# The order of the last two chunks, and a last store in two halves, in a streamed binary cross-entropy

## The chip, the cores and the metric

The kernel runs on one core of one Trainium2 chip. The metric is the device time of one execution in microseconds (us). The kernel before takes 1886.61 us (median of 3 runs, 1886.12 to 1887.61).

## The reference

Binary cross-entropy, element by element, on two arrays of 8192 x 8192 float32. The target holds only 0 and 1.

```python
def reference(pred, target):
    eps = 1e-7
    pred = np.clip(pred, eps, 1 - eps)
    return -(target * np.log(pred) + (1 - target) * np.log(1 - pred))
```

Because the target is 0 or 1, the result is -log|clip(pred) + (target - 1)|, and this is what the kernel computes: one logarithm for each element. 537 MB are read and 268 MB written.

## The kernel before

The 67.1 million elements are seen as one flat stream and cut into 37 chunks (k = 0 to 36, `last` = 36). A chunk has 128 partitions, with `FIRST` = 8192 columns in chunk 0 and `WIDE` = 14336 columns in all others. A row of a chunk is contiguous in memory: 57344 bytes of float32.

There are two buffers on the chip. `ring_p` holds three chunks in float32: the prediction is loaded there, worked on in place, and stored from there as the result. `ring_t` holds one chunk of the target in bfloat16; the load narrows it on the way. So the prediction of chunk k + 2 can be loaded only when the store of chunk k - 1 has landed, and the target of chunk k + 1 only when the merges of chunk k are done.

Compute works on halves of a chunk (`PARTS` = 2, 7168 columns; below, 36a and 36b are the halves of chunk 36). For each half:

- `clip` (L85): one VectorE instruction bounds the prediction.
- `merge` (L91, L94, L95): VectorE adds target - 1; ScalarE takes the absolute value and then the logarithm, in place.
- `negate` (L99): VectorE multiplies by -1.

The order is written out by hand: each engine executes its instructions in the order in which the program emits them, and a wait of one of them holds up all that stand behind it on that engine. VectorE's order for a chunk is merge a, merge b of chunk k; negate a, negate b of chunk k; clip a, clip b of chunk k + 1. ScalarE has absolute value and logarithm of a, then of b.

All big transfers are issued by GpSimd (POOL), in one queue and in program order: `load_t(k + 1)` (L67), `store(k)` (L70), `load_p(k + 2)` (L63). A wait of one of them holds up the later ones. Only the first load of the prediction is issued by ScalarE.

The end is special. The target of chunk 36 is loaded in two halves, and `store(34)` is issued behind these two loads. `store(35)` comes after the negations of chunk 35. The last store, `store_last`, writes columns 0 to 13311 of chunk 36 by one transfer on POOL's queue (L74), and the last `REST` = 1024 columns by three transfers on SyncE's queue (L77), of 108, 12 and 8 rows.

Of the kernel before, what the change touches and what calls it, by code (L numbers as in the profile page):

```python
# [1 line left out]

# [4 lines left out]

EPS = 1e-7

WIDE = 14336  # L10
FIRST = 8192
SLOTS = 3
PARTS = 2
REST = 1024
ROWS = (108, 12, 8)


@with_exitstack
def kernel(
    ctx: ExitStack,  # L20
    tc: tile.TileContext,
    pred: bass.AP,
    target: bass.AP,
    out: bass.AP,
):
    nc = tc.nc
    fp32 = mybir.dt.float32
    bf16 = mybir.dt.bfloat16
    Alu = mybir.AluOpType
    Act = mybir.ActivationFunctionType  # L30
    P = nc.NUM_PARTITIONS

    R, C = pred.shape
    total = R * C // P
    n = (total - FIRST) // WIDE + 1
    assert FIRST + (n - 1) * WIDE == total
    widths = [FIRST] + [WIDE] * (n - 1)
    last = n - 1

    pool = ctx.enter_context(tc.tile_pool(name="rings", bufs=1))  # L40
    ring_p = pool.tile([P, SLOTS * WIDE], fp32, name="ring_p", tag="ring_p")
    ring_t = pool.tile([P, WIDE], bf16, name="ring_t", tag="ring_t")
    warm = pool.tile([1, 8], fp32, name="warm", tag="warm")

    def chunk(ap, k):
        flat = ap.rearrange("r c -> (r c)")
        start = sum(widths[:k]) * P
        return flat[start : start + widths[k] * P].rearrange("(p w) -> p w", p=P)

    def p_of(k, a=0, b=None):  # L50
        c = k % SLOTS * WIDE
        return ring_p[:, c + a : c + (widths[k] if b is None else b)]

    def t_of(k, a=0, b=None):
        return ring_t[:, a : widths[k] if b is None else b]

    def part(k, i):
        w = widths[k]
        return i * w // PARTS, (i + 1) * w // PARTS

    def load_p(k):
        queue = nc.scalar if k == 0 else nc.gpsimd
        queue.dma_start(out=p_of(k), in_=chunk(pred, k))  # L63

    def load_t(k, *cols):
        cols = cols or (0, widths[k])
        nc.gpsimd.dma_start(out=t_of(k, *cols), in_=chunk(target, k)[:, cols[0] : cols[1]])  # L67

    def store(k):
        nc.gpsimd.dma_start(out=chunk(out, k), in_=p_of(k))  # L70

    def store_last():
        w = WIDE - REST
        nc.gpsimd.dma_start(out=chunk(out, last)[:, :w], in_=p_of(last, 0, w))  # L74
        r = 0
        for rows in ROWS:
            nc.sync.dma_start(  # L77
                out=chunk(out, last)[r : r + rows, w:], in_=p_of(last, w)[r : r + rows, :]
            )
            r += rows  # L80
        assert r == P

    def clip(k, i):
        p = p_of(k, *part(k, i))
        nc.vector.tensor_scalar(  # L85
            out=p, in0=p, scalar1=EPS, scalar2=1 - EPS, op0=Alu.max, op1=Alu.min
        )

    def merge(k, i):
        p, t = p_of(k, *part(k, i)), t_of(k, *part(k, i))  # L90
        nc.vector.scalar_tensor_tensor(  # L91
            out=p, in0=t, scalar=1.0, in1=p, op0=Alu.subtract, op1=Alu.add
        )
        nc.scalar.activation(out=p, in_=p, func=Act.Abs)  # L94
        nc.scalar.activation(out=p, in_=p, func=Act.Ln)  # L95

    def negate(k, i):
        p = p_of(k, *part(k, i))
        nc.vector.tensor_scalar(out=p, in0=p, scalar1=-1.0, scalar2=None, op0=Alu.mult)  # L99

    with tc.manual_schedule():
        load_p(0)
        load_t(0)
        load_p(1)
        nc.vector.memset(warm, 1.0)  # L105
        nc.scalar.activation(out=warm, in_=warm, func=Act.Ln)  # L106
        for i in range(PARTS):
            clip(0, i)
        for k in range(n):
            for i in range(PARTS):  # L110
                merge(k, i)
            if k < last - 1:
                load_t(k + 1)
            elif k == last - 1:
                load_t(last, 0, WIDE // PARTS)
                load_t(last, WIDE // PARTS, WIDE)
                store(last - 2)
            for i in range(PARTS):
                negate(k, i)
            if k < last:  # L120
                for i in range(PARTS):
                    clip(k + 1, i)
            if k < last - 2:
                store(k)
            if k < last - 1:
                load_p(k + 2)
        store(last - 1)
        store_last()


# [1 line left out]
_INS = ['pred', 'target']  # L132
_OUTS = [((8192, 8192), 'float32')]


# [23 lines left out]
```

## Time and profile before

| | |
|---|---|
| time, median of 3 runs | 1886.61 us |
| the profiled execution: its time | 1888.07 us |
| the profiled execution: its span | 1886.3 us |
| VectorE (DVE) busy | 1117.8 us, 59% |
| ScalarE (ACT) busy | 901.3 us, 48% |
| GpSimd (POOL) busy | 279.0 us, 15% |
| data moved by DMA | 671.14 MB, mean 356 GB/s |
| one clip, one merge on VectorE, one negation (7168 columns) | 3.85, 7.5, 3.85 us |
| one ScalarE pass (7168 columns) | 6.1 us |
| a store of one chunk, issue to landing | 31.1 us |

Times in the profile are in us from the span's start. A line of the timeline gives start, duration, engine, source line (L91 is line 91 of the kernel), operation, output and input with shape and type, how many instructions are merged into the line, and in brackets how long the engine sat idle before it and who released it. A line of the table by windows gives the stretch and its length, the busy time of VectorE, ScalarE and POOL with the number of instructions, the clock, the mean busy share of the 16 DMA engines and the GB/s they moved. `SPq` is SyncE's queue. The profile also records each packet that a DMA engine moves, with its size, start and duration, and each completion that a transfer writes.

### The profile page before, as it was taken

Reading aid. Unit: us, or ns where it says so; the run is one execution under the profiler, and the core shown is the slowest. Engines: PE = TensorE matmul, PEld = TensorE weight load, DVE = VectorE, ACT = ScalarE, POOL = GpSimd, SP = SyncE. Lnnn points to the kernel's source line nnn. Section 1 sums busy time; section 2 is a strip of 40 time slices with the busy share of each in tenths; the row PEclk is TensorE's granted clock in tenths of the full one; section 3 lists DMA queues with packets and bytes.
Section 4 is the critical chain, followed back from the end, with each engine's and each line's share of the span. In section 5 each row is a group of like instructions: output and inputs, shape, how many; then the busy total and the mean of one; then the engine's idle time right before and its main releaser. Section 6 shows DMA issues by size and latency. Waiting matters only on the chain.

```text
span 1886.3 us, 684 instructions
## 1 busy us (share of the span) xinstructions
DVE 1117.8 (59%) x223; ACT 901.3 (48%) x150; POOL 279.0 (15%) x115
## 2 busy tenths in 40 slices
DVE  4675566565555665556665655556655566666571
ACT  3555544444445555554444444555555544444453
POOL 0120111111111111011111111111100111111000
DMA  9999999999999999999999999999999999999994
GB/s 328 342 370 370 374 364 350 354 360 354 350 361 356 352 364 375 371 373 372 360 353 364 351 353 360 356 351 358 366 371 371 376 368 362 361 351 354 355 361 189
DMA packets 16293, 671.14 MB, mean 356 GB/s; under 512 B 1824, under 2 KB 1824, under 8 KB 1952
## 3 DMA queue, kind: packets, MB, share of 16 engines
q0 software_dynamic: 15984, 666.38, 98.4%
q10 hardware_dynamic: 144, 4.19, 0.6%
q1 hardware_dynamic: 160, 0.52, 0.1%
q14 instruction: 5, 0.04, 0.0%
HBM read 536.87 MB, written 268.44 MB: 427 GB/s over the span
## 4 chain that ended last, share of the span: by engine, by line
DMA 64%; issue 30%; DVE 2%; ACT 1%; POOL 1%; POOLq 0%; DVEq 0%; PEldq 0%
DMA ring_t<-in_target_dram 64%; DVE ring_p L91 2%; ACT ring_p L95 1%; ACT ring_p L94 1%; POOL out_dram L70 0%; DVE ring_p L99 0%; POOL ring_p L63 0%; POOLq L154 0%; POOLq L67 0%; POOL ring_t L67 0%; POOLq L70 0%; DVEq L91 0%; PEldq L154 0%; POOLq L74 0%
## 5 line engine op out<-in xcount | busy, mean ns | idle before, releaser
L94 ACT ACTIVATE ring_p<-ring_p 128x7168 f32<-128x7168 f32 (+1 forms) x74 | 451.4, 6100 | 952.0 <-DVE ring_p L91 952.0
L91 DVE SCALAR_TENSOR_TENSOR ring_p<-ring_t,ring_p 128x7168 f32<-128x7168 bf16 (+1 forms) x74 | 554.5, 7535 | 236.2 <-DMA ring_t<-in_target_dram 236.2
L99 DVE TENSOR_SCALAR ring_p<-ring_p 128x7168 f32<-128x7168 f32 (+1 forms) x74 | 285.0, 3851 | 486.5 <-ACT ring_p L95 486.5
L95 ACT ACTIVATE ring_p<-ring_p 128x7168 f32<-128x7168 f32 (+1 forms) x74 | 451.9, 6107 | 2.3
L85 DVE TENSOR_SCALAR ring_p<-ring_p 128x7168 f32<-128x7168 f32 (+1 forms) x74 | 281.6, 3847 | 19.4 <-DMA ring_p<-in_pred_dram 19.4
L70 POOL DMA_DIRECT2D out_dram<-ring_p x36 | 127.4, 3539 | 710.3 <-DVE ring_p L99 710.3
L67 POOL DMA_DIRECT2D ring_t<-in_target_dram x38 | 20.2, 531 | 830.8 <-DVE ring_p L91 830.0
L63 POOL DMA_DIRECT2D ring_p<-in_pred_dram x36 | 130.9, 3637 | 1.1 <-DMA out_dram<-ring_p 1.1
L74 POOL DMA_DIRECT2D out_dram<-ring_p x1 | 0.5, 531 | 40.1 <-DVE ring_p L99 40.1
L106 ACT ACT_TABLE_LOAD x1 | 1.3, 1283 | 1.1 <-PEq L143 1.1
L105 DVE MEMSET warm<- 1x8 f32 x1 | 0.1, 65 | 0.8 <-PEq L143 0.8
L106 ACT ACTIVATE warm<-warm 1x8 f32<-1x8 f32 x1 | 0.2, 207 | 0.0
L143 POOL MEMSET const-float32-0.0<- 128x1 f32 x1 | 0.1, 99 | 0.2 <-issue 0.2
L143 POOL MEMSET const-bfloat16-1.0<- 128x1 bf16 x1 | 0.1, 101 | 0.0
L143 POOL MEMSET const-uint8-127<- 128x1 uint8 x1 | 0.1, 99 | 0.0
L143 POOL MEMSET const-float32-1.0<- 128x1 f32 x1 | 0.1, 98 | 0.0
## 6 DMA issues: line engine op xcount, KB each, us to landing
ring_p<-in_pred_dram POOLq DMA_DIRECT2D x36, 7168.0 KB, 44.4
out_dram<-ring_p POOLq DMA_DIRECT2D x35, 7168.0 KB, 31.1
ring_t<-in_target_dram POOLq DMA_DIRECT2D x35, 3584.0 KB, 35.2
out_dram<-ring_p POOLq DMA_DIRECT2D x1, 6656.0 KB, 19.5
ring_p<-in_pred_dram ACTq DMA_DIRECT2D x1, 4096.0 KB, 19.5
out_dram<-ring_p POOLq DMA_DIRECT2D x1, 4096.0 KB, 21.3
ring_t<-in_target_dram POOLq DMA_DIRECT2D x2, 1792.0 KB, 17.9
ring_t<-in_target_dram POOLq DMA_DIRECT2D x1, 2048.0 KB, 21.4
```

The source lines that it names most:

```text
L63: queue.dma_start(out=p_of(k), in_=chunk(pred, k))
L67: nc.gpsimd.dma_start(out=t_of(k, *cols), in_=chunk(target, k)[:, cols[0] : cols[1]])
L70: nc.gpsimd.dma_start(out=chunk(out, k), in_=p_of(k))
L74: nc.gpsimd.dma_start(out=chunk(out, last)[:, :w], in_=p_of(last, 0, w))
L85: nc.vector.tensor_scalar(out=p, in0=p, scalar1=EPS, scalar2=1 - EPS, op0=Alu.max, op1=Alu.min)
L91: nc.vector.scalar_tensor_tensor(out=p, in0=t, scalar=1.0, in1=p, op0=Alu.subtract, op1=Alu.add)
L94: nc.scalar.activation(out=p, in_=p, func=Act.Abs)
L95: nc.scalar.activation(out=p, in_=p, func=Act.Ln)
L99: nc.vector.tensor_scalar(out=p, in0=p, scalar1=-1.0, scalar2=None, op0=Alu.mult)
L105: nc.vector.memset(warm, 1.0)
L106: nc.scalar.activation(out=warm, in_=warm, func=Act.Ln)
L143: nc = _bacc.Bacc("TRN2", target_bir_lowering=False, num_devices=1)
```

## The change

The loop over chunks ends two chunks earlier, with the same body. The last two chunks, 35 and 36, are written out:

- VectorE's order was: merge 35a, 35b; negate 35a, 35b; clip 36a, 36b; merge 36a, 36b; negate 36a, 36b. It becomes: merge 35a, 35b; clip 36a, 36b; negate 35a, merge 36a; negate 35b, merge 36b; negate 36a, 36b. ScalarE's order stays.
- POOL's order stays. `store(35)` now follows negate 35b in the new order.
- The last store's columns 0 to 13311 are written by two transfers instead of one: columns 0 to 7167, which wait for negate 36a, and columns 7168 to 13311, which wait for negate 36b. SyncE's three transfers are unchanged and wait for negate 36b.

The changed kernel has one line more above `clip`, so its line numbers from there on are higher by one.

```diff
     def store_last():
-        w = WIDE - REST
-        nc.gpsimd.dma_start(out=chunk(out, last)[:, :w], in_=p_of(last, 0, w))
+        half, w = WIDE // PARTS, WIDE - REST
+        for a, b in (0, half), (half, w):
+            nc.gpsimd.dma_start(out=chunk(out, last)[:, a:b], in_=p_of(last, a, b))
...
-        for k in range(n):
+        for k in range(last - 1):
             for i in range(PARTS):
                 merge(k, i)
-            if k < last - 1:
-                load_t(k + 1)
-            elif k == last - 1:
-                load_t(last, 0, WIDE // PARTS)
-                load_t(last, WIDE // PARTS, WIDE)
-                store(last - 2)
+            load_t(k + 1)
             for i in range(PARTS):
                 negate(k, i)
-            if k < last:
-                for i in range(PARTS):
-                    clip(k + 1, i)
+            for i in range(PARTS):
+                clip(k + 1, i)
             if k < last - 2:
                 store(k)
-            if k < last - 1:
-                load_p(k + 2)
+            load_p(k + 2)
+        for i in range(PARTS):
+            merge(last - 1, i)
+            load_t(last, *part(last, i))
+        store(last - 2)
+        for i in range(PARTS):
+            clip(last, i)
+        for i in range(PARTS):
+            negate(last - 1, i)
+            merge(last, i)
         store(last - 1)
+        for i in range(PARTS):
+            negate(last, i)
         store_last()
```

## Prediction

> **What bounds the kernel now.** I read the page first, then the timeline of the last 100 us, the table by windows of the tail, the transfers by issue, and the waits of SyncE's queue.
>
> ```profile
> DVE 1117.8 (59%) x223; ACT 901.3 (48%) x150; POOL 279.0 (15%) x115
> DMA  9999999999999999999999999999999999999994
> ```
>
> No compute engine is busy more than 59% of the span, and the DMA row is full in every slice but the last. The steady state is the DMA engines' own time, and the change does not touch it; what can change lies in that last slice (47 us). The timeline there:
>
> ```profile
> 1788.64 0.53 POOL L67 DMA_DIRECT2D ring_t<-in_target_dram  x1 [40.98 <-DVE ring_p L91]
> ...
> 1796.17 0.53 POOL L67 DMA_DIRECT2D ring_t<-in_target_dram  x1 [7.01 <-DVE ring_p L91]
> 1796.69 0.54 POOL L70 DMA_DIRECT2D out_dram<-ring_p  x1
> ...
> 1800.79 3.89 DVE L99 TENSOR_SCALAR ring_p<-ring_p 128x7168 f32<-128x7168 f32 x1 [4.92 <-ACT ring_p L95]
> ...
> 1813.07 3.90 DVE L99 TENSOR_SCALAR ring_p<-ring_p 128x7168 f32<-128x7168 f32 x1 [8.38 <-ACT ring_p L95]
> 1816.88 7.70 DVE L85 TENSOR_SCALAR ring_p<-ring_p 128x7168 f32<-128x7168 f32 x2
> 1817.26 3.62 POOL L70 DMA_DIRECT2D out_dram<-ring_p  x1 [20.03 <-DVE ring_p L99]
> 1824.50 15.14 DVE L91 SCALAR_TENSOR_TENSOR ring_p<-ring_t,ring_p 128x7168 f32<-128x7168 bf16 x2
> 1832.14 6.18 ACT L94 ACTIVATE ring_p<-ring_p 128x7168 f32<-128x7168 f32 x1 [19.10 <-DVE ring_p L91]
> ...
> 1856.83 3.89 DVE L99 TENSOR_SCALAR ring_p<-ring_p 128x7168 f32<-128x7168 f32 x1 [8.38 <-ACT ring_p L95]
> 1860.75 1.45 SPq L77 DMA_DIRECT2D out_dram<-ring_p  x3
> 1861.02 0.53 POOL L74 DMA_DIRECT2D out_dram<-ring_p  x1 [40.13 <-DVE ring_p L99]
> ```
>
> VectorE waits 4.92 and 8.38 us for the logarithms of chunk 35 before its two negations, and only then clips and merges chunk 36. So ScalarE sits idle 19.10 us before chunk 36 (at 1832.14), and the last store is issued at 1861.02. By windows:
>
> ```profile
> 1820.00:1842.00 22.00, 19.64 (x4) 9.83 (x2) 0.88 (x1) 1.00 0.98 425
> 1848.50:1862.50 14.00, 3.89 (x1) 8.26 (x2) 0.53 (x1) 1.00 0.06 17
> 1862.50:1880.50 18.00, 0.00 (x0) 0.00 (x0) 0.00 (x0) 1.00 0.94 395
> 1880.50:1886.30 5.80, 0.00 (x0) 0.00 (x0) 0.00 (x0) 1.00 0.00 0
> ```
>
> The last columns are DMA share and GB/s. Stores 34 and 35 run at 425 GB/s, then DMA is empty while the last chunk is computed, then the last store runs alone. SyncE's queue closes the span:
>
> ```profile
> SPq L154 <- DMA out_dram<-ring_p: 18.3, 1, 18.3
> ```
>
> It waits from 1862.2 to 1880.5 for the last landing; 5.8 us of closing work follow. The span therefore ends when the last store lands, and the hole in front of that store is what can be won.
>
> **The queue's own clock.** In the trace's packet records each of the 16 DMA engines carries 8 rows of a chunk: 8 packets of 57344 bytes, 2.12 us each, 16.9 us a store. The engines do not run level. Ten end store 35 at 1842.2 to 1842.8, six trail, at 1843.8, 1844.8, 1845.8, 1846.8, 1847.2 and 1848.0; the same staircase stands in store 34, 16.9 us earlier (1825.3 to 1831.1). It survives as long as the queue never empties. The last store's first packet starts at 1862.8, 1.7 us after its issue, and its completions come at 1879.1 to 1880.2, 6.1 us before the span's end.
>
> **The change, part by part.** I rebuild the tail with the durations above: clip 3.85 us (7.70 for two), negation 3.89, merge 7.6, each ScalarE pass 6.2, and 0.3 us from VectorE's end to POOL's issue.
>
> 1. Loads of the target halves. They keep their order in POOL's queue and their waits (each half of merge 35), so they stay at 1788.64 and 1796.17: cost nothing. They land 17.4 and 18.3 us later, at 1806.1 and 1814.5. Store 34, behind them, stays at 1796.7.
>
> 2. Clip 36 ahead of negation 35. This adds a wait: clip 36a needs chunk 36 of the prediction input, issued at 1747.13 and landing 50.4 us later, at 1797.5. VectorE is free at 1795.9, so it stalls 1.7 us; behind it wait both negations of chunk 35 and, on POOL, store 35. The clips run 1797.6 to 1805.3. Negation 35a, ready at 1800.8, now ends at 1809.2 instead of 1804.7.
>
> 3. Negations and merges in turn. Merge 36a runs 1809.2 to 1816.8 (its target half is there since 1806.1). Negation 35b follows (its logarithm ended at 1813.0) to 1820.7, then merge 36b to 1828.3. ScalarE starts chunk 36 at 1816.9 instead of 1832.1 and its four passes end at 1841.7; merge 36b is done 1 us before the third needs it. Negation 36a ends at 1833.2, 36b at 1845.6 instead of 1860.7: computing ends 15.1 us earlier.
>
> 4. Store 35. It moves past two clips and one merge: issued at 1821.0 instead of 1817.26. But there it spent 3.62 us on POOL beside a clip, against 0.53 for the issue beside a merge (1788.64) or an idle VectorE (1861.02). The new place lies beside merge 36b, so I take 0.53: done at 1821.5 against 1820.9. With 1.7 us to the first packet that is 1822.7, and the first engine needs it at 1825.3, when it ends store 34. Cost nothing, with a cover of 2.6 us; past that every us is paid in full. With 3.62 instead the first packet comes at about 1825.8, half a us late.
>
> 5. The two halves of the last store. The first is issued at 1833.5 and can flow from 1835.2; the first engine asks for it at 1842.2. The second is issued at 1845.9 and can flow from 1847.6; the first engine asks at 1842.2 + 8.5 = 1850.7 (cover 3.1 us). So the queue never empties. The trace has no store packet of 28672 or 24576 bytes, but chunk 0's 32768-byte packets took 1.21 us and the 57344-byte ones 2.12: along that line 1.06 and 0.91, which makes 8 x 1.97 = 15.8 us an engine, as the 53248-byte packets of today (1.97 each). Splitting adds no packet time.
>
> What does one more DMA cost in a full queue? Stores 34 and 35 land at 1831.5 and 1848.4, 16.9 us apart, which is 8 packets and nothing else. I take zero; the other end is the 1.7 us from issue to first packet paid again. The Trainium skill ("SBUF — State Buffer", section "The DMA setup-cost knee") speaks against splitting: every transfer pays roughly 2 us that do not scale with its bytes. By that rule the sum would end 2 us later; the two landings say it isn't paid while the queue holds work.
>
> 6. SyncE's three stores (128 packets of 4096 bytes at 0.16 us) move with negation 36b to 1845.6 and share the engines with the first half. Their 108, 12 and 8 rows go to 12, 12 and 8 engines (32 completion packets in the trace): at most 11 packets, 1.8 us, on an engine, none on four. Whether the most trailing engine is among the four, the trace does not tell: 0 to 1.8 us. I take 0.8.
>
> The end: the most trailing engine leaves store 35 at 1848.0, needs 15.8 us for its 16 packets and 0.8 for SyncE's rows: 1864.6. (The ten level ones end near 1842.8 + 15.8 + 1.8 = 1860.4.) With the 6.1 us of today's tail the span is 1870.7, 15.6 less than 1886.3. The profiled execution took 1888.07, 1.8 outside its span; the median of the runs is 1886.61. Taking 15.6 off the median gives **1871.0 us**. What is late next is the DMA queue itself, no longer any engine: about 3 us of extra compute delay would be free.
>
> Nearly all of this is the new order. With one undivided last store at 1845.9, the level engines would idle until 1847.6 and end at 1865.2, the trailing one at 1864.6: the halves bring about half a us here.
>
> **Rivals.**
>
> *A gap at each queue change* (faster, less so). If a further DMA costs its 1.7 us even with work queued, or POOL's issue of store 35 is held by VectorE, the end moves out by 1.7 to 2: 1872.7 to 1873. For it: an issue did take 3.62 beside a clip. Against it: the 16.9 us between landings.
>
> *The new wait ahead of negation 35 opens a hole* (faster, less so). If chunk 36 of the prediction input lands later than 1800.1, store 35 comes after its engines run dry and each us is lost. But it stands ahead of the target halves in the same queue, so by 1806.1 at the latest: 6 us at most, 1877.
>
> *Half-row packets cost as much as whole ones* (slower). Place: the 16 packets per engine of the last store. For it: the only 28672-byte packets in the trace, the target loads', took 2.13 us, as much as 57344-byte ones. At 2.13 the last store takes 34.1 us instead of 15.8, 18.3 more: 1889.3. It decides against the change from 1.95 us a packet up, where the 15.6 are used up. Against it: those packets read 57344 bytes of f32 and narrow them; 14336-byte ones took 1.08, 32768-byte stores 1.21.
>
> *The change does not do what it says*: the built queues rule most of this out, as VectorE's instructions stand in the new order with the waits named above, and the last store is two transfers. It could give nothing only if a wait covered both halves at once; then the time stays near 1886.
>
> **How the numbers follow.** Forecast as summed, 0.82; a gap, 0.08; the wait's hole, 0.04; packets too dear, 0.04; nothing, 0.02. The range: the bounds of SyncE's rows (0.8 down, 1.0 up), about 1 us between runs (1886.12 to 1887.61) and the gap's 2 us: 1868.0 to 1875.0, about 0.85 of the chance. A measurement here tells 0.2% (3.8 us) from no change. Faster 0.94, same 0.02, slower 0.04.
>
> **What would show it.** Right: ScalarE starts chunk 36 near 1817, negation 36b ends near 1846, the DMA share stays near 1 from 1842 to 1859 and falls off in a staircase to 1864.6, and SyncE's last wait ends there. Step 2 is wrong if VectorE's stall at 1796 is longer than 2 us; step 4 if the DMA share dips near 1825; step 5 if it dips near 1843 or 1851 or packets exceed 1.1 us; step 6 if completions come after 1866.

## The result, and the profile after

The changed kernel takes 1870.15 us (median of 5 runs, 1869.99 to 1870.96), against 1886.61 before: 16.5 us less, a ratio of 0.9911 with a 95% interval of 0.9897 to 0.9926. Its profiled execution has a span of 1869.2 us. The prediction was 1871.0, in a range of 1868.0 to 1875.0.

The page after has the same busy times of VectorE and ScalarE (1117.8 and 901.3 us), and in its row of DMA shares the last slice rises from 4 to 7:

```profile
DMA  9999999999999999999999999999999999999997
```

The timeline of the tail (start, duration, engine, line; line numbers from `clip` on are higher by one). VectorE, ScalarE and POOL run 2.3 us earlier in this execution than in the one before: the first half of the last target load is issued at 1786.36 instead of 1788.64. The first DMA engines do not: they end store 35 at 1842.4 against 1842.2.

```profile
1786.36 0.53 POOL L67 DMA_DIRECT2D ring_t<-in_target_dram  x1 [40.98 <-DVE ring_p L92]
...
1795.34 7.70 DVE L86 TENSOR_SCALAR ring_p<-ring_p 128x7168 f32<-128x7168 f32 x2 [1.74 <-DMA ring_p<-in_pred_dram]
...
1802.95 3.89 DVE L100 TENSOR_SCALAR ring_p<-ring_p 128x7168 f32<-128x7168 f32 x1
...
1806.75 7.62 DVE L92 SCALAR_TENSOR_TENSOR ring_p<-ring_t,ring_p 128x7168 f32<-128x7168 bf16 x1
1814.28 3.89 DVE L100 TENSOR_SCALAR ring_p<-ring_p 128x7168 f32<-128x7168 f32 x1
1814.40 6.18 ACT L95 ACTIVATE ring_p<-ring_p 128x7168 f32<-128x7168 f32 x1 [3.63 <-DVE ring_p L92]
...
1818.47 0.54 POOL L70 DMA_DIRECT2D out_dram<-ring_p  x1 [23.52 <-DVE ring_p L100]
...
1831.01 0.53 POOL L75 DMA_DIRECT2D out_dram<-ring_p  x1 [12.00 <-DVE ring_p L100]
...
1839.09 3.89 DVE L100 TENSOR_SCALAR ring_p<-ring_p 128x7168 f32<-128x7168 f32 x1 [8.38 <-ACT ring_p L96]
1843.02 1.73 SPq L78 DMA_DIRECT2D out_dram<-ring_p  x3
1843.28 0.53 POOL L75 DMA_DIRECT2D out_dram<-ring_p  x1 [11.74 <-DVE ring_p L100]
```

The reader sees the new wait (1.74 us ahead of the clips), ScalarE idle 3.63 us before chunk 36 instead of 19.10, store 35 issued in 0.54 us instead of 3.62, and the last negation ending at 1843.0. By windows (the last two columns are DMA share and GB/s):

```profile
1820.00:1842.00 22.00, 12.51 (x3) 19.00 (x4) 0.53 (x1) 1.00 0.99 427
1842.00:1848.00 6.00, 0.99 (x1) 0.00 (x0) 0.53 (x1) 1.00 0.92 394
1848.00:1859.00 11.00, 0.00 (x0) 0.00 (x0) 0.00 (x0) 1.00 0.99 426
1859.00:1863.40 4.40, 0.00 (x0) 0.00 (x0) 0.00 (x0) 1.00 0.34 145
1863.40:1869.20 5.80, 0.00 (x0) 0.00 (x0) 0.00 (x0) 1.00 0.00 0
```

The hole is gone. The DMA engines work through to 1859, fall off one after the other until 1863.2, and the closing part, from the last completion to the end of the span, is about as long as before (6.0 us against 6.1).

### The profile page after: what moved, and what is told of

Same layout as the page of the kernel before. It is cut to its first block, busy times and chain, and to the rows that moved or that the text cites. A ratio compares the mean times of both kernels' runs of the same rounds, so it can differ in the third digit from the quotient of the medians.

```text
span 1869.2 us, 685 instructions
## 1 busy us (share of the span) xinstructions
DVE 1117.8 (60%) x223; ACT 901.3 (48%) x150; POOL 276.4 (15%) x116
## 4 chain that ended last, share of the span: by engine, by line
DMA 65%; issue 28%; DVE 3%; ACT 2%; POOL 0%; another core or an unknown queue 0%; POOLq 0%; DVEq 0%; PEldq 0%
DMA ring_t<-in_target_dram 65%; DVE ring_p L92 2%; ACT ring_p L96 1%; ACT ring_p L95 1%; DVE ring_p L100 0%; DVE ring_p L86 0%; POOL out_dram L70 0%; POOL ring_p L63 0%; POOLq L159 0%; POOLq L67 0%; POOL out_dram L75 0%; POOLq L70 0%; DVEq L92 0%; PEldq L159 0%
```

## Experiments

Theory: the queue of the DMA engines sets the end, and the order of VectorE keeps it full. The cover of a store is the time by which it is ready before the first engine asks for it; the staircase is the spread between the first and the last of the 16 engines to end a transfer, and the trailing engine is that last one. Rivals: computing of the last chunk sets the end; the split of the store is what pays; each further transfer costs something of its own. The kernel before had medians of 1886.54, 1886.62 and 1885.71 us beside the three groups of runs below.

**The order alone (e1).** The last store undivided:

```diff
-        half, w = WIDE // PARTS, WIDE - REST
-        for a, b in (0, half), (half, w):
-            nc.gpsimd.dma_start(out=chunk(out, last)[:, a:b], in_=p_of(last, a, b))
+        w = WIDE - REST
+        nc.gpsimd.dma_start(out=chunk(out, last)[:, :w], in_=p_of(last, 0, w))
```

> The new order of VectorE with the last store undivided (columns 0 to 13311 in one transfer, waiting for negation 36b). Theory (the new order fills the hole; the trailing DMA engine sets the end): the store is issued near 1846 and can flow near 1847.5, when only the most trailing engine is still at store 35, so the time is 0 to 1.5 us above the changed kernel: 1870 to 1872. Rival (the two halves are what pays): the level engines idle for 5 us and the loss is a large part of the gain, 1875 or more.

Measured 1870.71 us (ratio 0.9914, 0.9900 to 0.9927), 15.8 less than the kernel before and 0.6 above the changed one. The order alone brings nearly all.

**The split alone (e2).** VectorE's old order with the halves:

```diff
-            clip(last, i)
-        for i in range(PARTS):
             negate(last - 1, i)
+        for i in range(PARTS):
+            clip(last, i)
+        for i in range(PARTS):
             merge(last, i)
```

> The old order of VectorE (negations 35, clips 36, merges 36) with the last store in two halves. Theory: negation 36a ends near 1848.5, its half flows from 1850.5 for 8.5 us, the second half is issued at 1861.0 as before and flows from 1862.7 for 7.3 us plus up to 1.8 us of SyncE's rows: the last landing comes 8.4 us before that of the kernel before, 1877 to 1879. Rival (order and halves add up, each about half): the same 8 us, but then the order alone must also give only 8.

Measured 1877.86 us (0.9956, 0.9943 to 0.9968): 8.7 us less than before. Its timeline shows the two halves far apart:

```profile
1847.03 0.53 POOL L75 DMA_DIRECT2D out_dram<-ring_p  x1 [27.86 <-DVE ring_p L100]
...
1859.31 0.53 POOL L75 DMA_DIRECT2D out_dram<-ring_p  x1 [11.75 <-DVE ring_p L100]
```

So the parts do not add up: 15.8 and 8.7 us alone, 16.5 together. Both fill the same hole, and behind the new order little of it is left for the halves.

**Early clips without turns (e3).** Both negations of chunk 35 stand ahead of both merges of chunk 36; the clips stay early:

```diff
         for i in range(PARTS):
             negate(last - 1, i)
+        for i in range(PARTS):
             merge(last, i)
```

> Clips 36 ahead of the negations of chunk 35, but no turns: negations 35a, 35b, then merges 36a, 36b; halves kept. Theory: merge 36a starts near 1817 (7.5 us earlier than in the kernel before, 7.6 later than in the changed one), negation 36b ends near 1853, the second half flows from 1855, 1 to 4 us after its engines ask: 1870.5 to 1873. If compute were what sets the end, the loss would be the whole 7.6 us: 1878.

Measured 1870.74 us (0.9914, 0.9900 to 0.9927).

```profile
1788.44 0.53 POOL L67 DMA_DIRECT2D ring_t<-in_target_dram  x1 [41.01 <-DVE ring_p L92]
...
1853.21 0.53 POOL L75 DMA_DIRECT2D out_dram<-ring_p  x1 [11.74 <-DVE ring_p L100]
```

Counted from the first half of the last target load, the last half is issued 64.8 us later instead of 56.9, 7.9 us more than in the changed kernel, and the median moves by 0.6 us. Computing does not set the end. In its profile, the slowest execution of the five (1873.76 us), the first engine ends the first half at 1850.8 and the last half's first packet starts at 1854.8, so the level engines do wait for it; the trailing one ends the first half only at 1856.2 and does not.

**Turns without early clips (e4).**

```diff
-        for i in range(PARTS):
-            clip(last, i)
         for i in range(PARTS):
             negate(last - 1, i)
+            clip(last, i)
             merge(last, i)
```

> Turns without the early clips: negation 35a, clip 36a, merge 36a, then the same for b; halves kept. Theory: the last negation ends within 2.5 us of the changed kernel's and the queue still never empties, so the time is the same within 0.5 us: 1869.7 to 1870.7. Rival (the early clips matter, since a clip between negation and merge delays ScalarE and store 35 is again issued beside a clip, 3.6 us on POOL): 2 to 4 us slower, 1872 to 1874.

Measured 1871.39 us (0.9919, 0.9905 to 0.9932), between the two expectations. As the rival said, store 35 is again issued beside a clip:

```profile
1819.11 3.63 POOL L70 DMA_DIRECT2D out_dram<-ring_p  x1 [23.02 <-DVE ring_p L100]
```

But that opens no hole: the first engines complete store 34 at 1825.2 and store 35 at 1842.1, 16.9 us apart. Where the 1.2 us lie is not shown. The most trailing engine of this execution left store 35 at 1846.9 instead of 1845.7, and that differs from execution to execution (below). Together e3 and e4 say that, with the halves, either part of the new order, the early clips or the turns, brings nearly all of the gain; with neither (e2) it is 8.7 us.

**Delaying the last half (e5, e6).** One (e5) and two (e6) more absolute values on ScalarE for half 36b. The cut shows e6; e5 has `range(2 ...)`:

```diff
-        nc.scalar.activation(out=p, in_=p, func=Act.Abs)
+        for _ in range(3 if (k, i) == (last, PARTS - 1) else 1):
+            nc.scalar.activation(out=p, in_=p, func=Act.Abs)
```

> The changed kernel with one more absolute value on ScalarE for the last half chunk (36b), which changes no value and delays its logarithm, its negation, the last half store and SyncE's rows by 6.2 us. Theory (the queue sets the end; computing runs ahead of it by about 3 us for the level engines and 6 for the trailing one): 0 to 0.8 us slower, 1870 to 1871. Rival (computing of the last half sets the end): 6 us slower, 1876.

> The same with two more absolute values, 12.4 us of delay. Theory: the cover is used up; the last half flows from about 1857.4 on all engines at once, and ends 7.3 us plus up to 1.8 us later: 1866.5 to 1867.5 instead of 1863.3, so 3 to 4.5 us slower than the changed kernel, 1873.2 to 1874.7. Rival: 12 us slower, 1882.

With one pass 1870.23 us (0.9918, 0.9904 to 0.9932): 6.2 us of extra computing cost 0.1. With two 1874.83 us (0.9939, 0.9927 to 0.9952): 12.4 us cost 4.7, slightly above the expected end of 4.5. The windows tell why; first one pass, then two:

```profile
1850.00:1858.00 8.00, 0.00 (x0) 0.00 (x0) 0.00 (x1) 1.00 0.98 396
```

```profile
1850.00:1858.00 8.00, 3.89 (x1) 2.23 (x1) 0.53 (x1) 1.00 0.23 88
```

With one pass the engines are still busy at 0.98 in this stretch, with two they run dry. This is the clearest evidence for the theory: the price of a delay is what is left of it after the queue's cover.

**Halves in all stores (e7).**

```diff
-        nc.gpsimd.dma_start(out=chunk(out, k), in_=p_of(k))
+        for i in range(PARTS):
+            a, b = part(k, i)
+            nc.gpsimd.dma_start(out=chunk(out, k)[:, a:b], in_=p_of(k, a, b))
```

> The changed kernel with each of the 36 other chunk stores cut into two half-row transfers as well, one behind the other. Theory (a further transfer in a full queue costs nothing, and half rows cost half): the same time within 1.5 us. Rival 1 (1.7 us for each further transfer, as from issue to first packet in an empty queue): 36 x 1.7 = 61 us slower, 1931. By the Trainium skill (SBUF - State Buffer, The DMA setup-cost knee) it would be 36 x 2 = 72 us, 1942; no other number here rests on this.

Measured 1874.55 us (0.9935, 0.9920 to 0.9950): 4.4 us slower than the changed kernel, outside the 1.5 us of the theory, and far from 1931 and 1942. A further transfer in this full queue adds 4.4 / 36 = 0.12 us to the time, not 1.7. The rule of the Trainium skill ("SBUF — State Buffer", "The DMA setup-cost knee"), some 2 us for each transfer whatever its size, does not show here, where the next transfer is already queued. The lines for VectorE's merges waiting for the target (us in all, times, longest), of the changed kernel and of this one, show that the queue did lose time:

```profile
DVE ring_p L92 <- DMA ring_t<-in_target_dram: 234.0, 34, 7.7
```

```profile
DVE ring_p L94 <- DMA ring_t<-in_target_dram: 241.0, 34, 8.0
```

That is 7.0 us over the run, but not all of it belongs to the transfers. In the twelve other profiles, whose loop is the same, this sum is 232.9 to 237.6 us, and it is large where the staircase at store 35 is wide: 232.9 with 2.8 us in e1, 237.6 with 6.5 us in e8. In e7 the staircase is 6.8 us wide, so e8 is the nearer comparison, and against it e7 waits 3.4 us longer, an estimate of 0.1 us a transfer. Whether the additional transfers also widen the staircase is not shown. The last completion stands at 1870.3, 7.1 us later than in the changed kernel, but the span ends 2.8 us after it instead of 6.0, so the time does not show the whole delay.

**No stores by SyncE (e8).** The second half store takes all its 7168 columns:

```diff
-        half, w = WIDE // PARTS, WIDE - REST
+        half, w = WIDE // PARTS, WIDE
         for a, b in (0, half), (half, w):
             nc.gpsimd.dma_start(out=chunk(out, last)[:, a:b], in_=p_of(last, a, b))
-        r = 0
-        for rows in ROWS:
-            nc.sync.dma_start(
-                out=chunk(out, last)[r : r + rows, w:], in_=p_of(last, w)[r : r + rows, :]
-            )
-            r += rows
-        assert r == P
```

> The changed kernel without SyncE's three stores: the second half store takes all 7168 columns of its half. Theory (the trailing engine carried 11 of SyncE's rows, 1.7 us, where an even share of the same bytes is 1.2): each engine gets 17.0 us of packets behind store 35 instead of 15.8 plus 0 to 1.8, so 0 to 1 us faster, 1869.2 to 1870.2. Rival (SyncE's rows lie on engines that finish early, so they are free): the trailing engine gets 1.2 us more, 1871.3.

Measured 1871.82 us (1870.50 to 1875.09; ratio 0.9924, 0.9912 to 0.9937). The expected gain is not there and the median lies nearer to the rival's 1871.3, but the interval overlaps that of the changed kernel, so the sign of this small effect is not settled. The arithmetic of one engine holds: in its profile the last completion of store 35 comes at 1850.3 and the last of all at 1867.3, the 17.0 us expected. But this profiled execution is the slowest of the five (1875.09 us), its trailing engine began 4.6 us later than in the changed kernel's profile, and that hides half a us.

**The closing part (e9, e10, e11).** Tiny memsets on POOL at the start, 12, 40 and 100 of them, to see whether POOL's place in its instruction stream explains the shorter closing part of e7:

```diff
+    pad = pool.tile([1, 8], fp32, name="pad", tag="pad")
...
+        for _ in range(12):
+            nc.gpsimd.memset(pad, 0.0)
```

> The changed kernel with 12 tiny memsets on POOL at the start (in idle time, about 0.1 us each), to move its later instructions 12 places on. In the run with halves everywhere the closing part, from the last completion to the end of the span, took 2.9 us instead of 6.0, with POOL's closing drain 2.8 us shorter. Theory (where POOL's closing instructions lie in its stream decides): one of 12, 40 or 100 places brings a closing of 2.9 us and 1867.3; the others change nothing, 1870.2. Rival (the number of transfers decides): closing 6.0 us and 1869.7 to 1870.9 in all three.

> The same with 40 memsets. Theory: a closing of 2.9 us here, in the run with 12 or in that with 100. Rival: 6.0 us, 1869.7 to 1870.9.

> The same with 100 memsets (10 us of POOL's idle time before its third transfer). Theory: a closing of 2.9 us here or in the runs with 12 or 40. Rival: 6.0 us, 1869.7 to 1870.9.

Measured 1870.84, 1871.30 and 1870.68 us (0.9918, 0.9904 to 0.9933; 0.9920, 0.9905 to 0.9935; 0.9926, 0.9909 to 0.9943), with 5.7 us from the last completion to the end of the span in all three. None of the three places brings the short closing part, so that theory falls; why e7 closes in 2.8 us stays open. No kernel here had a median below that of the changed one.

## Why the prediction was right, point by point

*What bounds the kernel.* Shown. With VectorE's order alone the time falls by 15.8 us, and 6.2 us of additional computing are then free.

*Steps 1 to 3.* The stall on the new wait was put at 1.7 us and measured 1.74. Counted from the first half of the last target load, computing ends 15.5 us earlier (56.6 us after it instead of 72.1); 15.1 were predicted.

*Step 4.* Store 35's issue took 0.54 us beside a merge. Completions of store 34 begin at 1825.5 and of store 35 at 1842.4, so no hole opened. The cover was larger than the 2.6 us given: issued at 1818.47, the store can flow from 1820.2, and the first engine asks at 1825.5, 5.3 us later. In e4 an issue of 3.63 us opens no hole either, but this does not test the half us that was estimated for that end: counted from the first half of the last target load, e4's store is issued at 31.6 us and its first engine asks at 37.7, where the prediction had 32.4 and 36.7.

*Step 5.* The half rows took 1.06 and 0.91 us a packet, to the hundredth as the straight line through the two known sizes gave them; the rival of packets that cost as much as whole ones is out. A further transfer costs 0.1 us (e7), near the zero taken. The 1.7 us from issue to first packet are no constant: in e2 the first half, issued at 1847.03 with no store of SyncE's beside it, starts at 1848.13, 1.1 us later, and the last half, with those stores beside it, 1.7 us after its issue. The forecast time does not use this term; the covers do. That the halves bring about half a us fits e1 (0.6), though the intervals do not tell it from zero. The cover for computing was given as about 3 us, and e5 shows that 6.2 us are free. The cover hangs on the staircase: computing follows the last engine's landing, and the first engine asks first. In the profile after, the staircase is 3.3 us wide instead of 5.8; the last half can flow from 1843.3 + 1.7 = 1845.0, and the first engine asks at 1842.4 + 8.5 = 1850.9, a cover of 5.9 us instead of 3.1. In e5 the first engine ends the first half at 1850.3, SyncE's rows begin at 1850.3 and the last half at 1851.0, so the rows fill the rest.

*Step 6 and the end.* Two terms were mis-sized, in opposite directions. The trailing engine was to leave store 35 at 1848.0 and left it at 1845.7. SyncE's rows were to cost it 0.8 us; from there to the last completion of all, at 1863.2, it is 17.5 us, 15.8 and 1.7, near the upper bound given. (The completions do not name their engine; that the same one is last both times is assumed.) In e9, e10 and e11, the same kernel with memsets ahead, the second term is 1.4, 1.3 and 1.5 us, and in e7 0.3, so this term too differs between executions. Together the last completion came 1.4 us before the 1864.6 predicted, and with the 6.0 us of closing (6.1 predicted) the span ended at 1869.2, 1.5 us below the 1870.7 of the sum. The median ended 0.85 us below the forecast. That the number is this close is in part luck: the two errors partly offset each other, and the profiled execution before was 1.5 us above its median, the one after 0.8.

*The weak point* was to take one execution's staircase as a constant. From first to last completion of store 35 it is 5.8 us wide in the profile before, 3.3 in the one after, 2.8 in e1 and 6.5 in e8. The range covered this, but the text had not named it as a bound.

## What to carry to other kernels

When the transfers bound a kernel, look for the one stretch in which their queue runs empty, and order the compute so that each result is ready before the engines ask for it; beyond that, earlier results bring nothing. Two edits that fill the same hole do not add up, so cost the second on top of the first. And count the queue's end by the engine that trails, not by the mean of the 16.

## What the runs showed of the hardware that was not expected

- The 16 DMA engines drift apart while the queue never empties, but not steadily. In the profile before, the first and the last completion of one transfer stand 0.6 us apart near 100 us, 3.2 near 507, 4.6 near 914 and 5.8 at the end; in the one after 0.6, 3.0, 3.3 and 3.3. Where the queue stays full to the end, the trailing engine sets the end; its lag is paid in the loop too, as VectorE's wait for the target is 232.9 us in e1 and 237.6 in e8. The width in store 35 was between 2.8 us (e1) and 6.8 (e7). Behind the empty queue of the kernel before it is back at 1.1. What makes an engine fall behind, the runs don't show.
- From the last completion to the end of the span it is 5.7 to 6.1 us in all profiles but that of e7, which has 36 more transfers and takes 2.8.
